# RWKV-7 keys transposed by VectorE and DMA instead of TensorE, in a two-layer streaming encoder step on one core

## The chip, the cores and the metric

One core of one Trainium2 chip runs the whole step. The metric is the device time of an execution in microseconds; the time given for the kernel before is the median of 3 executions. A profiled execution of the same kernel is looked at beside it.

## What is computed

The step has two layers over 512 prompt tokens and 32 sample tokens of width 1024, in float32. Layer 0 mixes tokens by RWKV-7 (24 heads of 64), layer 1 by differential attention; both also attend to a memory of 256 rows, multiply by a SiLU gate and project back. The change lies in layer 0. Its recurrence, per head, is

```python
def step(S, inp):
    r_t, k_t, v_t, w_t, kk_t, a_t = inp
    sa = jnp.einsum('bhvk,bhk->bhv', S, -kk_t)
    S = (S * w_t[:, :, None, :] + sa[..., None] * (kk_t * a_t)[:, :, None, :]
         + v_t[..., None] * k_t[:, :, None, :])
    return S, jnp.einsum('bhvk,bhk->bhv', S, r_t)
```

followed by a normalization of each head's output y (its mean taken off, then its variance), a bonus term, and the gate. The prompt starts from a zero state, the sample from `state_rwkv`; both last states are outputs.

## The kernel before

**Tiling.** The recurrence is done in chunks of 64 tokens: 8 for the prompt, and the sample's 32 tokens as a ninth. Two heads make a pair, so that 128 partitions are full; there are 12 pairs. For a pair, `rw_prep` turns projected rows into decayed queries and keys: `zr` and `bk` (features on partitions, tokens along the free dimension), the decay at each chunk's end `dl`, and the chunk matrices `at`. `rw_invert`, `rw_back`, `rw_at` and `rw_merge` invert the chunk matrices on GpSimd through DRAM scratch (`sc`, `m`). `rw_chain` runs `chunk` 8 times: each chunk reads the state `SB`, makes two matmuls into `ps_c`, an update `avz` by VectorE, a copy `sv` by ScalarE, then a matmul of `sv` with `bt` and the new `SB` by VectorE. This is the recurrence: three hops per chunk that wait for each other. `bt` is `bk` turned, tokens on partitions: for each half of the prompt (512 columns), four 128x128 transposes on TensorE into `ps_bt` and one copy `bt<-ps_bt` by ScalarE (lines 827 to 846). `rw_sample` does the same for the sample chunk, from a state `SS` that it loads at its begin (l. 994), transposes on TensorE (`ps_si`) and copies (`ssi`). `rw_finish` normalizes `yt`: `gs` is the sum over a head, scaled by 1/64, then subtracted.

**The projection in between.** TensorE's main work is the input projection `ps_g` (128x272 outputs). Each weight block of 1024x128 is loaded in two halves (`raw`), and split into a high part `whi` (a rounding copy by ScalarE) and a low part `wlo` (a subtraction by VectorE), so that a product is three matmuls in a row: `hh,whi`, `hl,whi`, `hh,wlo`, each half block 12 of them per half of the tokens. `stream` (in `layer0`) loads two blocks ahead and splits one ahead.

**What sets the order.** All engines work through queues in program order, and the program order is written by a planner in `layer0`. The main loop goes over the pairs; `PLAN` (l. 49) has 23 rows per pair with two halves each. A row issues one hop of the pair's recurrence and then the listed steps, for example `("prep", 2, 0, 0.42)`: the next step of `rw_prep` for the pair two ahead, with 0 us declared for TensorE and 0.42 us for VectorE. Between the steps it issues projection matmuls until a due time is reached. The steps of `rw_prep` are counted off by its `yield`s; the table says where each falls. A pair's last steps of `prep` come a pair or less ahead of its own chain: distance 2 in rows 13 to 15 and 0 to 14, distance 1 in rows 0 to 4 of the next pair.

The splits are deferred: `put_off` appends them to a list with 0.75 us declared for `wlo` (`LATER`) and 0 for `whi`, and `some` takes one from the list's head at the end of each half row, a `wlo` only if the room reckoned from the declared VectorE costs so far allows it (or if more than four wait). When a block's matmuls begin, `until(todo[-1][0])` issues whatever of that block's splits still stands in the list, at that place:

```python
    if self.later and 0 < self.later[0][1] <= room and self.place_no > self.acted + 1:
        fn, us = self.later.pop(0)
        fn()
...
    spent += self.some(room * (k + (half + 1) / 2) + 0.4 - spent)
```

SyncE issues nearly all DMAs, in order; a DMA whose data isn't ready holds up those behind it. Before the loop, three start-up stages (`FILL0` to `FILL2`) prepare pairs 0, 1 and 2 with projection blocks between. At pair 9 the kernel keeps back 24 projection steps (`KEPT`) for three last `prep` steps of pair 11.

All operations go through one helper (`tie`, l. 106), so the profile gives line 106 for nearly all, and they are told apart by the tiles' names.

Of the kernel before, what the change touches and what calls it, by code (L numbers as in the profile page):

```python
# [9 lines left out]
F32 = mybir.dt.float32  # L10
# [39 lines left out]
    [[("val", 0, 0.95, 0), ("prep", 2, 0.1, 0)], [("prep", 2, 0, 0.42)]],  # L50
# [14 lines left out]
    [[("fin", -1, 0, 0.98), ("smp", 0, 0.11, 0)], [("prep", 2, 0.4, 0), ("prep", 3, 0, 0.6)]],  # L65
# [8 lines left out]
SHIFTED, KEPT = 13, 24  # L74
# [34 lines left out]
class Trunk:  # L109
# [535 lines left out]
    def rw_prep(self, st, rkv):  # L645
# [73 lines left out]
        self.ve.tensor_copy(dl[:, :8], ch(de[:])[:, :, 64])  # L719
        self.ve.tensor_copy(dl[:, 8:9], de[:, CU - 1 : CU])  # L720
# [105 lines left out]
        self.ae.copy(sv[2][:TS, 0, :], ps[P - TS :, P : 2 * P])  # L826
        for q in range(2):
            yield
            if q:
                ps = self.psm.tile([P, 512], F32, tag="m", name="ps_v")  # L830
                for i in range(4):
                    self.te.transpose(ps[:, i * P : i * P + P], v[:, i * P : i * P + P], self.ident[:])
                pv = ps[:].rearrange("p (j c) -> p j c", j=4)
                for u in range(2):
                    if u:
                        yield
                    sv[u] = self.rb.tile([P, 4, P], F32, tag="sv", name="sv", bufs=4)
                    self.ae.copy(sv[u][:64, 0:4:2, :], pv[:64, 2 * u : 2 * u + 2])
                    self.ae.copy(sv[u][64:, 1:4:2, :], pv[64:, 2 * u : 2 * u + 2])
                yield  # L840
            ps = self.psm.tile([P, 512], F32, tag="m", name="ps_bt")
            for j in range(4):
                c = 4 * q + j
                self.te.transpose(ps[:, j * P : j * P + P], bk[:, c * P : c * P + P], self.ident[:])
            bt[q] = self.rb.tile([P, 4, P], F32, tag="bt", name="bt", bufs=4)
            self.ae.copy(bt[q][:], ps[:].rearrange("p (j c) -> p j c", j=4))
# [146 lines left out]

    def rw_sample(self, st):
# [3 lines left out]
        for h in range(2):  # L998
            self.se.dma_start(sl[64 * h : 64 * h + 64, 64 * h : 64 * h + 64], self.a["state_rwkv"][0, 0, 2 * pr + h])
# [1308 lines left out]
```

## Time and profile before

| what | value |
|---|---|
| median of 3 executions | 1348.16 us (1347.06 to 1348.51) |
| profiled execution, its own time | 1349.83 us |
| its span, first to last instruction | 1348.1 us |
| mean granted TensorE clock | 0.997 |
| TensorE matmul busy | 1319.8 us, 98% |
| VectorE busy | 956.5 us, 71% |
| ScalarE busy | 813.1 us, 60% |
| GpSimd busy | 368.0 us, 27% |
| moved by DMA | 150.47 MB, mean 112 GB/s |

The profile comes from one execution; its span is 1.7 us shorter than that execution's time. A row of a timeline has the start in us from the span's begin, the duration in us, the engine, the line, the operation and its tiles (output, then inputs), shapes, the count of equal instructions in the row, and in brackets, where the engine stood idle just before, how long and what released it. Matmuls overlap in TensorE's pipeline: the time that one costs the queue is the distance to the next one's start, not its duration. The layer-0 main loop lies at about 130 to 620 us, and a pair takes some 43.7 us of it (the same `wlo` starts at 236.67 and 280.29 us in two pairs that follow each other).

### The profile page before, as it was taken

The page shows a single profiled execution, that of the slowest core. Times are in us where ns is not written, and L with a number is a line of the kernel's source. Part 1 is how long each engine was busy: PE and PEld are TensorE (multiplying, and loading weights), DVE is VectorE, ACT ScalarE, POOL GpSimd, SP SyncE. Part 2 cuts the span into 40 slices and gives each one's busy share as a digit, 9 for nine tenths or more (in the row PEclk, how much of TensorE's full clock was granted, in tenths as well). Part 3 has the DMA queues.
Part 4 walks back from the last instruction along what each step waited for, and adds up shares of the span by engine and source line. Part 5 has one row for each costly group of instructions (what it writes and reads, how often), then busy time and mean ns, then how long its engine had stood idle before and what let it go on. Part 6 is the DMA issues. An engine that isn't in the chain of part 4 may idle for free. (4 is left out here: it accounts for less than half of the span.)

```text
span 1348.1 us, 31624 instructions
## 1 busy us (share of the span) xinstructions
PE 1319.8 (98%) x11662; PEld 1264.6 (94%) x11662; DVE 956.5 (71%) x2391; ACT 813.1 (60%) x2258; POOL 368.0 (27%) x833
## 2 busy tenths in 40 slices
PE   8999999999999999999999999999999999999997
PEld 6988899999999998988999999999999999999997
DVE  5766878888887888675764578876588748887343
ACT  5766777877787777665543366754476546664222
POOL 2128668666776677600000000000000001002000
PEclk9999999999999999999999999999999999999999
DMA  7443322333233322342465466652367424762321
GB/s 225 145 138 76 82 57 68 85 87 92 59 96 87 75 78 70 100 124 83 115 188 138 130 192 149 145 141 79 98 154 160 110 83 108 164 148 89 94 86 68
DMA packets 370805, 150.47 MB, mean 112 GB/s; under 512 B 163177, under 2 KB 361202, under 8 KB 370650
## 3 DMA queue, kind: packets, MB, share of 16 engines
q1 hardware_dynamic: 370586, 148.43, 42.0%
q8 instruction: 92, 1.51, 0.5%
q14 instruction: 63, 0.52, 0.1%
q10 hardware_dynamic: 64, 0.02, 0.0%
HBM read 118.00 MB, written 30.18 MB: 110 GB/s over the span
## 5 line engine op out<-in xcount | busy, mean ns | idle before, releaser
L106 PE MATMUL ps_g<-hh,wlo 128*128 128x272 f32 x1808 | 536.1, 297 | 1.1 <-DVE wlo L106 1.0
L106 PE MATMUL ps_g<-hh,whi 128*128 128x272 f32 x1808 | 533.9, 296 | 1.0 <-DVE ats L106 0.7
L106 PE MATMUL ps_g<-hl,whi 128*128 128x272 f32 x1808 | 532.7, 295 | 1.0 <-DVE hl L106 0.7
L106 PEld LDWEIGHTS ps_g<-hh,whi 128*128 128x128 f32 x1808 | 341.1, 189 | 5.9 <-DVE ats L106 0.9
L106 PEld LDWEIGHTS ps_g<-hl,whi 128*128 128x128 f32 x1808 | 340.9, 189 | 3.9 <-DVE hl L106 1.9
L106 PEld LDWEIGHTS ps_g<-hh,wlo 128*128 128x128 f32 x1808 | 340.5, 189 | 3.0 <-DVE wlo L106 1.8
L106 DVE TENSOR_TENSOR wlo<-raw,whi 128x512 fp32r<-128x512 f32 x314 | 214.4, 693 | 106.3 <-ACT whi L106 102.0
L106 ACT CAST whi<-raw 128x512 fp32r<-128x512 f32 x314 | 188.9, 619 | 116.7 <-PE ps_g L106 64.9
L868 POOL TENSOR_TENSOR tm<-u,m 102x84 f32<-102x84 f32 (+23 forms) x341 | 138.8, 407 | 117.6 <-DMA m<-sc 71.2
L870 POOL TENSOR_TENSOR u<-u,tm 102x84 f32<-102x84 f32 (+23 forms) x341 | 158.5, 465 | 26.7
L106 PE MATMUL ps_g<-hi,wlo 128*128 128x272 f32 x512 | 147.8, 289 | 1.1 <-DVE wlo L106 1.1
L106 PE MATMUL ps_g<-hi,whi 128*128 128x272 f32 x512 | 147.7, 288 | 0.0
L106 PE MATMUL ps_g<-lo,whi 128*128 128x272 f32 x512 | 147.4, 288 | 0.0
L1339 POOL TENSOR_TENSOR lo<-og,hi 128x544 fp32r<-128x544 f32 x8 | 13.2, 1651 | 378.1 <-ACT hi L106 377.6
L106 PEld LDWEIGHTS ps_g<-hi,wlo 128*128 128x128 f32 x512 | 96.4, 188 | 1.6 <-DVE wlo L106 1.5
L106 PEld LDWEIGHTS ps_g<-hi,whi 128*128 128x128 f32 x512 | 96.6, 189 | 0.0
L106 PEld LDWEIGHTS ps_g<-lo,whi 128*128 128x128 f32 x512 | 96.4, 188 | 0.0
L106 ACT ACTIVATE pt<-ps_s,snm 128x128 f32<-128x128 f32 (+3 forms) x96 | 50.3, 527 | 57.1 <-DVE snm L106 57.1
L106 DVE SCALAR_TENSOR_TENSOR SB<-ps_c,dl,sd 64x64 f32<-64x64 f32 x168 | 47.4, 282 | 26.6 <-PE ps_c L106 20.9
L106 ACT COPY sv<-ps_c 64x64 f32<-64x64 f32 x192 | 39.6, 206 | 33.1 <-PE ps_c L106 31.2
L1803 POOL MEMSET qs<- 128x128 f32 x2 | 0.3, 206 | 188.9 <-PE ps_g L106 188.9
L106 ACT ACTIVATE sg<-ps_g 128x272 f32<-128x272 f32 x64 | 25.1, 394 | 40.2 <-PE ps_g L106 36.2
(397 smaller groups left out, 2523.1 us busy)
## 6 DMA issues: line engine op xcount, KB each, us to landing
raw<-in_rw_in_dram SPq DMA_DIRECT2D x114, 256.0 KB
raw<-in_df_in_dram SPq DMA_DIRECT2D x112, 256.0 KB
raw<-in_w_out_dram SPq DMA_DIRECT2D x64, 256.0 KB
oscr<-sg SPq DMA_DIRECT2D x16, 272.0 KB
lo<-oscr SPq DMA_DIRECT2D x16, 272.0 KB
m<-sc SPq DMA_DIRECT2D x33, 128.0 KB
raw<-in_w_mem_v_dram SPq DMA_DIRECT2D x16, 256.0 KB
out_dram<-kt SPq DMA_DIRECT2D x48, 64.0 KB
```

The costliest lines, as they stand in the source:

```text
L106: return lambda *a, **k: self.trunk.tie(self, issue(*a, **k))
L868: nc.gpsimd.tensor_tensor(tm[:, :n, :wd], u3[:, :n, kx : kx + 1].to_broadcast(sh), m3[:, kx : kx + 1, kx + 1 :].to_broadcast(sh), ALU.mult)
L870: nc.gpsimd.tensor_tensor(u3[:, :n, kx + 1 :], u3[:, :n, kx + 1 :], tm[:, :n, :wd], ALU.add)
L1339: (self.nc.gpsimd if g % 2 and self.o1 else self.ve).tensor_tensor(lo[:], t, hi[:].bitcast(F32), ALU.subtract)
L1803: nc.gpsimd.memset(t[:], 0.0)
```

## The change

The eight prompt chunks' `bk` is no longer transposed on TensorE. VectorE transposes each half in squares of 32x32 within its 128x512 (two `STREAM_TRANSPOSE` per pair, row 0 of the pair before it is used). Each square is then right in itself but in the wrong place; four DMAs (`tscr<-bt`, one for each 32 partitions, 128-byte pieces) write the squares to DRAM where they belong, and one DMA (`bt<-tscr`) reads the whole 512 KB back. The writes are issued in row 0 right behind the transposes, the read-back in row 7. The copies `bt<-ps_bt` by ScalarE go with the transposes. `PLAN` declares 1.42 us of VectorE for the new step in place of 0.42 for the step that copied `dl`, and drops the two steps of rows 4 and 15 that held the TensorE transposes.

Besides, the `dl` and `ssi` copies move from VectorE to ScalarE; the scaling of `gs` is folded into the subtraction; the sample state `SS` is loaded in row 19 of the pair before; and the kept steps at pair 9 come in four portions instead of three.

```diff
--- before.py
+++ after.py
@@ -47,14 +47,14 @@
-    [[("val", 0, 0.95, 0), ("prep", 2, 0.1, 0)], [("prep", 2, 0, 0.42)]],
+    [[("val", 0, 0.95, 0), ("prep", 2, 0.1, 0)], [("prep", 2, 0, 0), ("prep", 1, 0, 1.42)]],
...
-    [[("smp", 0, 0.11, 0.28), ("prep", 1, 0.4, 0)], [("prep", 2, 0, 0.86)]],
+    [[("smp", 0, 0.11, 0.28)], [("prep", 2, 0, 0.86)]],
...
@@ -71,7 +71,7 @@
-SHIFTED, KEPT = 13, 24
+SHIFTED, ASKED, KEPT = 13, 19, 24
@@ -716,8 +716,8 @@
-        self.ve.tensor_copy(dl[:, :8], ch(de[:])[:, :, 64])
-        self.ve.tensor_copy(dl[:, 8:9], de[:, CU - 1 : CU])
+        self.ae.copy(dl[:, :8], ch(de[:])[:, :, 64])
+        self.ae.copy(dl[:, 8:9], de[:, CU - 1 : CU])
@@ -824,26 +824,29 @@
         bt[2] = self.rb.tile([P, 1, P], F32, tag="bts", name="bts", bufs=2)
         self.ae.copy(bt[2][:, 0, :], ps[:, :P])
         self.ae.copy(sv[2][:TS, 0, :], ps[P - TS :, P : 2 * P])
+        yield
+        scr = self.dp.tile([2 * TP, P], F32, tag="tscr", name="tscr", bufs=2)
+        tb = self.rb.tile([P, 8, P], F32, tag="bt", name="bt", bufs=2)
+        bt[:2] = tb[:, :4], tb[:, 4:]
         for q in range(2):
-            yield
-            if q:
-                ps = self.psm.tile([P, 512], F32, tag="m", name="ps_v")
-                for i in range(4):
-                    self.te.transpose(ps[:, i * P : i * P + P], v[:, i * P : i * P + P], self.ident[:])
-                pv = ps[:].rearrange("p (j c) -> p j c", j=4)
-                for u in range(2):
-                    if u:
-                        yield
-                    sv[u] = self.rb.tile([P, 4, P], F32, tag="sv", name="sv", bufs=4)
-                    self.ae.copy(sv[u][:64, 0:4:2, :], pv[:64, 2 * u : 2 * u + 2])
-                    self.ae.copy(sv[u][64:, 1:4:2, :], pv[64:, 2 * u : 2 * u + 2])
+            self.ve.transpose(bt[q].rearrange("p j c -> p (j c)"), bk[:, q * TP : q * TP + TP])
+        to = scr[:].rearrange("(b i) (a c) -> a i b c", i=TS, c=TS)
+        for a in range(4):
+            u = slice(TS * a, TS * a + TS)
+            self.se.dma_start(to[a], tb[u].rearrange("i j c -> i (j c)").rearrange("i (b c) -> i b c", c=TS))
+        yield
+        ps = self.psm.tile([P, 512], F32, tag="m", name="ps_v")
+        for i in range(4):
+            self.te.transpose(ps[:, i * P : i * P + P], v[:, i * P : i * P + P], self.ident[:])
+        pv = ps[:].rearrange("p (j c) -> p j c", j=4)
+        for u in range(2):
+            if u:
                 yield
-            ps = self.psm.tile([P, 512], F32, tag="m", name="ps_bt")
-            for j in range(4):
-                c = 4 * q + j
-                self.te.transpose(ps[:, j * P : j * P + P], bk[:, c * P : c * P + P], self.ident[:])
-            bt[q] = self.rb.tile([P, 4, P], F32, tag="bt", name="bt", bufs=4)
-            self.ae.copy(bt[q][:], ps[:].rearrange("p (j c) -> p j c", j=4))
+            sv[u] = self.rb.tile([P, 4, P], F32, tag="sv", name="sv", bufs=4)
+            self.ae.copy(sv[u][:64, 0:4:2, :], pv[:64, 2 * u : 2 * u + 2])
+            self.ae.copy(sv[u][64:, 1:4:2, :], pv[64:, 2 * u : 2 * u + 2])
+        yield
+        self.se.dma_start(tb[:], scr[:].rearrange("(j p) c -> p j c", p=P))
 
     def rw_invert(self, st):
 
@@ -991,17 +994,20 @@
             S, Sn = SB[c % 2], SB[(c + 1) % 2]
             yield from self.chunk(st, c, S, Sn)
 
+    def state_in(self, pr):
+
+        for h in range(2):
+            self.se.dma_start(self.SS[0][64 * h : 64 * h + 64, 64 * h : 64 * h + 64], self.a["state_rwkv"][0, 0, 2 * pr + h])
+
     def rw_sample(self, st):
 
         nc, p, pr = self.nc, self.rb2, st["pr"]
         sl = self.SS[0]
-        for h in range(2):
-            self.se.dma_start(sl[64 * h : 64 * h + 64, 64 * h : 64 * h + 64], self.a["state_rwkv"][0, 0, 2 * pr + h])
         yield
         ps = self.psm.tile([P, 4, P], F32, tag="m", name="ps_si")
         self.te.transpose(ps[:, 0, :], sl[:], self.ident[:])
         S = p.tile([P, P], F32, tag="ssi", name="ssi", bufs=1)
-        self.ve.tensor_copy(S[:], ps[:, 0, :])
+        self.ae.copy(S[:], ps[:, 0, :])
         yield from self.chunk(st, 8, S, sl)
         yield
         self.state_out(sl, self.o[8][0, 0, 2 * pr : 2 * pr + 2])
@@ -1097,10 +1103,9 @@
         y = yt[:].rearrange("p i (h v) -> p (i h) v", h=2)
         s = p.tile([P, 10], F32, tag="gs", name="gs", bufs=1)
         self.ve.tensor_reduce(s[:], y, AX.X, ALU.add)
-        self.ve.tensor_scalar(s[:], s[:], 1.0 / 64, None, ALU.mult)
         sh = [P, 10, 64]
         yield
-        self.ve.tensor_tensor(y, y, s[:].unsqueeze(2).to_broadcast(sh), ALU.subtract)
+        self.ve.scalar_tensor_tensor(y, s[:].unsqueeze(2).to_broadcast(sh), -1.0 / 64, y, ALU.mult, ALU.add)
         yield
         sq = p.tile([P, 10, 64], F32, tag="gsq", name="gsq", bufs=1)
         self.ae.activation(sq[:], y, AF.Square)
@@ -1615,6 +1620,7 @@
                 go(kind, 0)
                 fill(n)
             ready = len(FILL2) - 12
+            self.state_in(0)
             each[0] -= sum(map(sum, (FILL0, FILL1, FILL2, FILL3))) - 4 * 24 - 6 * 48
             for pr in range(NPAIR):
                 mplan = MPLAN.get(pr, ())
@@ -1648,6 +1654,8 @@
                                 t += MEMPE / 12
                         if half and pr == LAM and k in (1, 7):
                             (self.lam_in if k == 1 else self.lam_out)()
+                        if half and pr + 1 < NPAIR and k == ASKED:
+                            self.state_in(pr + 1)
                         if half and pr == NPAIR - 2 and k == SHIFTED:
                             self.shift_out()
                         if half and pr == NPAIR - 2 and k % 2 and len(came) < EARLY:
@@ -1665,9 +1673,9 @@
                     next(main)
                     left -= 1
                 if pr + 3 == NPAIR:
-                    for _ in range(3):
+                    for _ in range(4):
                         go("prep", pr + 2)
-                        fill(KEPT // 3)
+                        fill(KEPT // 4)
                     while self.later:
                         self.later.pop(0)[0]()
                     ca.close()
```

Three places of the queues follow. The first is VectorE's queue in a pair of the main loop, around rows 6 to 8 of the plan: `at` and `ats` are the chunk matrices, `SB` the state, `SS` the sample's state, `avz` the recurrence's update, `wlo` the low part of a weight half, `sg` a gate. Before:

```order
L106 TENSOR_TENSOR at_1695<-ps_at,mk 128x4x2x64 [waits PE_49] x2
L106 TENSOR_TENSOR avz<-ps_c,avz 64x128 [waits PE_49]
L106 TENSOR_TENSOR wlo<-raw,whi 128x512 [waits DMAHW4_49,Activation_49]
L106 TENSOR_TENSOR at_1695<-ps_at,mk 128x4x2x64 [waits PE_49] x2
L106 TENSOR_TENSOR ats<-ps_ats,mk 128x2x64 [waits PE_49] x2
L106 SCALAR_TENSOR_TENSOR SB_540<-ps_c,dl,sd 64x64 [waits PE_49,Activation_49]
L106 SCALAR_TENSOR_TENSOR SB_540<-ps_c,dl,sd 64x64
L106 SCALAR_TENSOR_TENSOR SS<-ps_c,dl,sd 64x64 [waits DMAHW6_49,PE_49]
L106 SCALAR_TENSOR_TENSOR SS<-ps_c,dl,sd 64x64 [waits DMAHW7_49]
L106 TENSOR_TENSOR avz<-ps_c,avz 64x128 [waits PE_49]
L106 TENSOR_TENSOR wlo<-raw,whi 128x512 [waits DMAHW5_49]
```

and in the changed kernel:

```order
L106 TENSOR_TENSOR at_1691<-ps_at,mk 128x4x2x64 [waits PE_49] x2
L106 TENSOR_TENSOR avz<-ps_c,avz 64x128 [waits PE_49]
L106 TENSOR_TENSOR at_1691<-ps_at,mk 128x4x2x64 [waits PE_49] x2
L106 TENSOR_TENSOR ats<-ps_ats,mk 128x2x64 [waits PE_49] x2
L106 SCALAR_TENSOR_TENSOR SB_540<-ps_c,dl,sd 64x64 [waits PE_49,Activation_49]
L106 SCALAR_TENSOR_TENSOR SB_540<-ps_c,dl,sd 64x64
L106 SCALAR_TENSOR_TENSOR SS<-ps_c,dl,sd 64x64 [waits DMAHW3_49,PE_49]
L106 SCALAR_TENSOR_TENSOR SS<-ps_c,dl,sd 64x64 [waits DMAHW4_49]
L106 TENSOR_TENSOR avz<-ps_c,avz 64x128 [waits PE_49]
L106 TENSOR_TENSOR wlo<-raw,whi 128x512 [waits DMAHW6_49]
L106 TENSOR_TENSOR wlo<-raw,whi 128x512 [waits DMAHW7_49,Activation_49]
```

The `wlo` that stood between `avz` and the second pair of `at` now stands behind the next `avz`, directly ahead of the block's other half. TensorE's third matmul of that block has a wait for VectorE there now; before it had none.

The second place is VectorE's queue some 13 us later in the same pair, rows 16 to 18: `q` and `nt` belong to a reciprocal square root, `yt` is the output being normalized, `bv` the bonus term. Before:

```order
L106 SCALAR_TENSOR_TENSOR q_101<-nt,q_101 128x26 [waits DVE_49]
L106 TENSOR_TENSOR yt_1689<-yt_1689,q_101 128x640 [waits DVE_49]
L106 TENSOR_TENSOR wlo<-raw,whi 128x512 [waits Activation_49]
L106 SCALAR_TENSOR_TENSOR SB_541<-ps_c,dl,sd 64x64 [waits PE_49,Activation_49]
L106 SCALAR_TENSOR_TENSOR SB_541<-ps_c,dl,sd 64x64
L106 MEMSET cum 128x9
L106 SCALAR_TENSOR_TENSOR bv_1690<-ps_y,PA,bv_1690 128x512 [waits PE_49]
L106 SCALAR_TENSOR_TENSOR bv_1690<-ps_y,PA,bv_1690 128x32 [waits PE_49]
L106 TENSOR_TENSOR avz<-ps_c,avz 64x128 [waits PE_49]
L106 TENSOR_TENSOR wlo<-raw,whi 128x512 [waits DMAHW7_49,Activation_49]
```

and in the changed kernel:

```order
L106 SCALAR_TENSOR_TENSOR q_101<-nt,q_101 128x26 [waits DVE_49]
L106 TENSOR_TENSOR wlo<-raw,whi 128x512 [waits Activation_49]
L106 TENSOR_TENSOR yt_1685<-yt_1685,q_101 128x640 [waits DVE_49]
L106 TENSOR_TENSOR wlo<-raw,whi 128x512 [waits DMAHW0_49,Activation_49]
L106 SCALAR_TENSOR_TENSOR SB_541<-ps_c,dl,sd 64x64 [waits PE_49,Activation_49]
L106 SCALAR_TENSOR_TENSOR SB_541<-ps_c,dl,sd 64x64
L106 MEMSET cum 128x9
L106 SCALAR_TENSOR_TENSOR bv_1686<-ps_y,PA,bv_1686 128x512 [waits PE_49]
L106 SCALAR_TENSOR_TENSOR bv_1686<-ps_y,PA,bv_1686 128x32 [waits PE_49]
L106 TENSOR_TENSOR avz<-ps_c,avz 64x128 [waits PE_49]
```

The `wlo` that stood behind `avz` now stands ahead of `yt`, and two stand between `nt` and `SB` where one stood.

The third place is SyncE's queue in the start-up: `m` and `sc` belong to the inverse of pair 0, `raw` are halves of weight blocks, `memt` and `mkv` memory keys. Before:

```order
L106 DMA m_1165<-sc_1146 32x1024
L106 DMA m_1165<-sc_1146 2x1024
L106 DMA raw<-in_rw_in_dram 128x4x128 x2
L106 DMA out_dram<-memt 128x2x128
L106 DMA mkv_781<-memt 128x256
L106 DMA raw<-in_rw_in_dram 128x4x128 x2
```

and in the changed kernel:

```order
L106 DMA m_1165<-sc_1146 32x1024
L106 DMA m_1165<-sc_1146 2x1024
L106 DMA tscr<-bt 32x32x32 x4
L106 DMA bt<-tscr 128x8x128
L106 DMA raw<-in_rw_in_dram 128x4x128 x2
L106 DMA out_dram<-memt 128x2x128
L106 DMA mkv_781<-memt 128x256
L106 DMA raw<-in_rw_in_dram 128x4x128 x2
```

The four scratch writes and the read-back for pair 0 stand ahead of a load of weights. In the main loop the writes stand ahead of a load of weights too, and the read-back two loads later.

More of the change, by code (lines that the diff above doesn't have):

```diff
@@ L53 @@
     [[("prep", 2, 0, 0)], [("prep", 2, 0, 1.0)]],
-    [[("smp", 0, 0.11, 0.28), ("prep", 1, 0.4, 0)], [("prep", 2, 0, 0.86)]],
+    [[("smp", 0, 0.11, 0.28)], [("prep", 2, 0, 0.86)]],
     [[("out", -1, 0.11, 0)], [("prep", 2, 0, 0.84)]],
     [[("prep", 2, 0, 1.1), ("smp", 0, 0.21, 0.29)], [("prep", 2, 0, 0.86)]],
-    [[("prep", 2, 1.1, 1.37)], [("smp", 0, 0.21, 0)]],
+    [[("prep", 2, 1.1, 1.37)], [("smp", 0, 0.21, 0), ("prep", 1, 0, 0)]],
     [[], [("prep", 2, 0, 0.9), ("prep", 2, 1.1, 1.37)]],
@@ L64 @@
     [[("prep", 2, 0.25, 0)], []],
-    [[("fin", -1, 0, 0.98), ("smp", 0, 0.11, 0)], [("prep", 2, 0.4, 0), ("prep", 3, 0, 0.6)]],
+    [[("fin", -1, 0, 0.98), ("smp", 0, 0.11, 0)], [("prep", 3, 0, 0.6)]],
     [[("prep", 3, 0.53, 0), ("mrg", 1, 0, 0.86)], []],
```

## The prediction

> **What bounds the kernel now.** I read the page's engine totals first, then the table by stretches for the layer-0 main loop (about 130 to 620 us, where most of the change acts).
>
> ```profile
> span 1348.1 us, 31624 instructions
> PE 1319.8 (98%) x11662; PEld 1264.6 (94%) x11662; DVE 956.5 (71%) x2391; ACT 813.1 (60%) x2258; POOL 368.0 (27%) x833
> ...
> L106 PE MATMUL ps_g<-hh,wlo 128*128 128x272 f32 x1808 | 536.1, 297 | 1.1 <-DVE wlo L106 1.0
> ```
>
> ```profile
> 250.00:300.00 50.00, 50.00 (x549) 47.64 (x549) 42.15 (x105) 38.41 (x112) 35.39 (x74) 1.00 0.28 72
> ```
>
> In the stretch from 250 to 300 us the columns are PE, PEld, DVE, ACT, POOL, granted clock, DMA share, GB/s: TensorE is busy for all 50.00 us at clock 1.00, VectorE for 42.15, ScalarE for 38.41. So TensorE's issue is the bound: work taken from it shortens the stage, and any wait put into its queue lengthens it, unless a pause is already there. The group's line on the page says that in the whole run TensorE waits only 1.0 us for wlo, the low half of a split weight. That will matter: the planner gives VectorE's splits their places.
>
> **What TensorE is relieved of.** The 24 groups of four transposes go. To see their worth I read TensorE's timeline at two groups of one pair, by the starts of neighbours, not by durations, since matmuls overlap.
>
> ```profile
> L106 PE MATMUL ps_bt<-ident,bk x96: 270/272/330, 83.1 to 562.0; 128*128 128x128 f32 x96
> ```
>
> ```profile
> 222.83 0.27 PE L106 MATMUL ps_si<-ident,SS 128*128 128x128 f32 x1
> 222.94 0.60 PE L106 MATMUL ps_bt<-ident,bk 128*128 128x128 f32 x4
> 223.29 0.37 PE L106 MATMUL ps_g<-hh,whi 128*128 128x272 f32 x1
> ...
> 244.54 0.60 PE L106 MATMUL ps_bt<-ident,bk 128*128 128x128 f32 x4
> 244.90 0.37 PE L106 MATMUL ps_g<-hl,whi 128*128 128x272 f32 x1
> 245.11 0.29 PE L106 MATMUL ps_g<-hh,wlo 128*128 128x272 f32 x1
> ```
>
> The first group takes 223.29 - 222.94 = 0.35 us of issue. ps_si stays ahead of it, so the longer step into the main projection (0.21 us instead of about 0.125) stays too. The second stands alone between projection matmuls: 0.36 us, and the step 245.11 - 244.90 = 0.21 falls by 0.085, together 0.445. Twelve pairs: 12 x 0.35 + 12 x 0.445 = **9.5 us gained**. The durations would promise more: 24 groups of 0.60 us are 14.4.
>
> [...]
>
> **First new wait: a split forced at the block's start.** The order shows VectorE's queue changed beyond what the diff names. Once per pair, in pairs 1 to 8, the first-half wlo of a projection block stood after an avz at row 6; now it stands behind the next avz, directly ahead of its second half, because the higher VectorE cost declared for row 0 (1.42 in place of 0.42) leaves a deferred split less room at that place, and the block's start then forces what is left. These are the rows of before, TensorE and then VectorE.
>
> ```profile
> 235.85 0.46 PE L106 MATMUL ps_c<-SB,zr 128*128 128x128 f32 x2
> 236.06 0.37 PE L106 MATMUL ps_g<-hh,wlo 128*128 128x272 f32 x1
> 236.27 0.29 PE L106 MATMUL ps_g<-hh,whi 128*128 128x272 f32 x1
> 236.40 0.29 PE L106 MATMUL ps_g<-hl,whi 128*128 128x272 f32 x1
> 236.53 0.29 PE L106 MATMUL ps_g<-hh,wlo 128*128 128x272 f32 x1
> ```
>
> ```profile
> 231.35 0.67 DVE L106 TENSOR_TENSOR wlo<-raw,whi 128x512 fp32r<-128x512 f32 x1
> ...
> 236.34 0.29 DVE L106 TENSOR_TENSOR avz<-ps_c,avz 64x128 f32<-64x128 f32 x1
> 236.67 0.69 DVE L106 TENSOR_TENSOR wlo<-raw,whi 128x512 fp32r<-128x512 f32 x1
> ```
>
> The block's third matmul, at 236.53, reads that wlo, done since 232.0 in before. In the new order the split comes where the second-half wlo stands now, at 236.67, behind an avz that waits for the ps_c of 235.85. It ends at 236.67 + 0.69 = 237.36; TensorE wants it at 236.53. That is a wait of 0.83 us, or 0.96 with the 0.13 us that a hand-over from VectorE can take (252.83 to 252.96, below). Everything in TensorE's queue stands behind it, and so does the recurrence. I take 0.9 us x 8 pairs = **7.2 us lost** (bounds 0 if a pause elsewhere absorbed it, and 7.7; rows of before show no such pause).
>
> **Second new wait: a split ahead of the state.** A wlo that stood at 254.03, after the state update, now goes ahead of yt, in pairs 1 to 7.
>
> ```profile
> 246.10 0.58 DVE L106 SCALAR_TENSOR_TENSOR SB<-ps_c,dl,sd 64x64 f32<-64x64 f32 x2 [1.25 <-PE ps_c L106]
> ...
> 250.77 0.83 DVE L106 TENSOR_TENSOR yt<-yt,q 128x640 f32<-128x640 f32 x1
> 251.51 0.83 DVE L106 TENSOR_TENSOR wlo<-raw,whi 128x512 fp32r<-128x512 f32 x1
> 252.26 0.57 DVE L106 SCALAR_TENSOR_TENSOR SB<-ps_c,dl,sd 64x64 f32<-64x64 f32 x2
> ...
> 254.03 0.67 DVE L106 TENSOR_TENSOR wlo<-raw,whi 128x512 fp32r<-128x512 f32 x1
> ```
>
> ```profile
> 252.84 0.29 PE L106 MATMUL ps_g<-hh,whi 128*128 128x272 f32 x1
> 252.96 0.42 PE L106 MATMUL ps_c<-SB,zr 128*128 128x128 f32 x2
> ```
>
> VectorE waits for TensorE ahead of the SB at 246.10, and from there no row has an idle time up to the SB that ends at 252.83. TensorE's ps_c follows at 252.96, just one matmul step after 252.84: no margin, but no wait yet. One more split costs its step, 252.26 - 251.51 = 0.75 us; leaving a hand-over's few hundredths of slack, 0.7 us x 7 = **4.9 us lost** (0 to 5.3).
>
> **What VectorE, ScalarE and the queue take on.** For the squares the trace has a layer-1 transpose of the same 128x512 shape, on row 0 of the next pair an idle time, and behind it the copies that leave.
>
> ```profile
> L106 DVE STREAM_TRANSPOSE kt<-k x12: 711/711/711, 811.9 to 1196.8; 128x512 f32<-128x512 f32 x12
> ```
>
> ```profile
> 215.40 0.24 DVE L106 COPY dl<-de 128x8 f32<-128x8 f32 x2
> 217.47 0.58 DVE L106 TENSOR_SCALAR SB<-ps_c,dl 64x64 f32<-64x64 f32 x2 [1.82 <-PE ps_c L106]
> ...
> 261.09 0.58 DVE L106 TENSOR_SCALAR SB<-ps_c,dl 64x64 f32<-64x64 f32 x2 [1.71 <-PE ps_c L106]
> ```
>
> Two transposes take 2 x 0.711 = 1.42 us and stand right ahead of that SB. The idle time is 1.71 to 1.82, and the dl copies (0.24) leave it: some 0.5 us of cover remains, so I cost them at nothing; without the cover it would be 1.42 x 11 = 16 us. The copies given to ScalarE (dl, ssi) go against its 24 dropped copies of ps_bt; it has 11.6 of 50 us free. The dropped scaling of gs and the earlier state load are off the path: nothing.
>
> On SyncE's queue, four scratch writes (128 KB each, in 128-byte pieces) now stand ahead of a weight load in every pair and wait for the transposes. Rows of before, the load and the split that needs it, and the nearest small-piece writes with the read that waits for them:
>
> ```profile
> 258.26 1.14 SPq L106 DMA_DIRECT2D raw<-in_rw_in_dram  x2
> ...
> 829.66 3.42 SPq L106 DMA_DIRECT2D ascr<-og  x4
> 833.19 1.01 SPq L106 DMA_DIRECT2D raw<-in_df_in_dram  x2
> 834.67 0.37 SPq L106 DMA_DIRECT2D og<-ascr  x1
> ```
>
> ```profile
> 271.64 0.60 ACT L106 CAST whi<-raw 128x512 fp32r<-128x512 f32 x1
> ```
>
> The transposes end before 261.1; the writes' issue takes up to 3.42 us, so the load goes out near 264.5 instead of 258.26, 7.1 us ahead of its use. The read-back is asked for seven rows after the writes, and has most of a pair until it is used. Both hidden: nothing, with a few tenths per pair at the worst in the range.
>
> [...]
>
> In the start-up there is less room. For pair 0 the writes and the read-back stand together, ahead of a weight load; these are the queue, then its reader, then TensorE.
>
> ```profile
> 84.08 2.02 SPq L106 DMA_DIRECT2D m<-sc  x6
> 86.20 1.30 SPq L106 DMA_DIRECT2D raw<-in_rw_in_dram  x2
> ```
>
> ```profile
> 94.48 0.62 ACT L106 CAST whi<-raw 128x512 fp32r<-128x512 f32 x1
> ```
>
> ```profile
> 84.54 0.66 PE L106 MATMUL ps_v<-ident,rkv 128*128 128x128 f32 x4 [0.59 <-ACT svs L106]
> ...
> 99.11 0.73 PE L106 MATMUL ps_b<-r,hs 128*128 128x128 f32 x5 [0.72 <-ACT r L106]
> ```
>
> Issuing four writes takes 1.35 us at the pitch of the m reads (2.02 us for six) and up to 3.42 by the row of ascr; waiting until they have landed takes 834.67 - 833.08 = 1.6 us or more; the read-back's issue 0.4. The load leaves 3.4 to 5.4 us late, with 2.9 to 4.9 us until its use at 94.48. ScalarE would stand there with the start of pair 0 behind it (r, for which TensorE already waits at 99.11). Bounds: a gain of 0.6 (the wait at 84.54 goes with the ps_bt copies) to a loss of 5.4; I take a net loss of **1.4 us**, since the load has most of the time it needs.
>
> **The sum.** -9.5 + 7.2 + 4.9 + 1.4 = +4.0 us. The profiled execution took 1349.83 us (1.7 more than its span); 1353.8 of that kind is 1348.16 + 4.0 = **1352.2 us** against the median.
>
> **The rivals.** (1) *The relief is kept*: one of the two split waits is absorbed, by a place where the recurrence, not the issue, sets TensorE's pace. For it: the 24 groups surely go. Against it: rows of before show no pause of 0.7 us after either place. With the first wait gone, 1352.2 - 7.2 = 1345.0; with both, 1340.1. Chance 0.19. This one ends faster; it decides from the point where over 6.7 us of the waits are absorbed. (2) *Nearly nothing*: the start-up costs nothing and the waits come out at their lower prices, 0.83 x 8 + 0.6 x 7 = 10.8 against 9.5 + 0.6: +0.7, or 1348.9 us. Chance 0.28. (3) *Transfers*: the scratch writes land so slowly that the weight load misses its use in every pair. Each microsecond past the 7.1 costs 11 us in 11 pairs: 1352.2 + 11 = 1363. For it: the start-up load in before was issued 8.3 us ahead of its use, so no row proves 7.1 enough. Against it: a DMA share of 0.28. Chance 0.10. (4) *Durations count*: 14.4 instead of 9.5 is gained, 1352.2 - 4.9 = 1347.3; the 0.35 us between neighbours speaks against it. Chance 0.03. [...] That the transposes don't leave TensorE can't be: the new order has none.
>
> **How the numbers follow.** My forecast has 0.40, and its own range is 1351 to 1356. A measurement of this kernel tells 0.2%, 2.7 us, from no change, so faster is below 1345.5 and slower above 1350.9. Faster is rival 1 and a sliver of rival 4: 0.20. Same is rival 2 and the rest of rival 4: 0.30. Slower is the forecast and rival 3: 0.50. The range reaches into rival 1 and over rival 2, and leaves out 1340 and the far transfers: 1342 to 1358.
>
> **What would show it.** Right: no ps_bt rows; in each of pairs 1 to 8 a matmul ps_g<-hh,wlo with an idle time of about 0.9 us released by DVE wlo, and the group's 1.1 us of idle time grown to about 8; in pairs 1 to 7 a ps_c<-SB with 0.7 us of idle time released by DVE SB; TensorE busy under 50 of 50 us in every stretch of the loop; the SB at the pair's begin still with idle time ahead of it. Wrong: these waits at under 0.3 us, a pair shorter than before by 0.8 us, or waits for DMA raw on ScalarE inside the loop.

## The result, and the profile after

| kernel | median | ratio to before, 95% interval |
|---|---|---|
| before | 1348.34 us (4 runs) | |
| changed | 1366.68 us (1364.55 to 1368.89, 4 runs) | 1.0137 (1.0118 to 1.0157) |

The change costs 18.5 us (15.9 to 21.2), on the side that was forecast, but 14.5 us more than forecast and outside the range. These are the head of the changed kernel's page and the group of matmuls that need the low halves of weights.

```profile
span 1366.9 us, 31492 instructions
PE 1318.2 (96%) x11566; PEld 1259.5 (92%) x11566; DVE 964.0 (71%) x2367; ACT 806.7 (59%) x2270; POOL 356.9 (26%) x833
...
L106 PE MATMUL ps_g<-hh,wlo 128*128 128x272 f32 x1808 | 540.7, 300 | 6.9 <-DVE wlo L106 6.7
```

TensorE is busy for 96% in place of 98%: its busy time fell by 1.6 us and the span grew by 18.8. The idle time ahead of the low-half matmuls rose from 1.1 to 6.9 us, as the order had said. That is a third of the loss. The list of TensorE's waits names the rest: engine, tile and line, what it waited for, us in total, times, the longest.

```profile
PE ps_g L106 <- DVE wlo L106: 8.1, 12, 1.0
PE ps_b L106 <- ACT r L106: 5.8, 1, 5.8
PE ps_ck L106 <- DMA cmt<-in_cache_mem_k_dram: 5.4, 1, 5.4
...
PE ps_y L106 <- DVE yt L106: 1.4, 5, 0.4
```

Two single waits of 5.8 and 5.4 us stand there, once each in the run. To see when the time is lost I compared the starts of the same instruction in both traces (changed minus before, us):

| instruction, its start in before | lag |
|---|---|
| ps_rt of pair 0's preparation, 96.9 | -0.3 |
| ps_s of pair 1's preparation, 119.0 | +6.3 |
| ps_si of pair 1, 179.1 | +5.9 |
| ps_si of pair 8, 485.5 | +11.1 |
| ps_bts of pair 11's preparation, 545.7 | +12.8 |
| ps_si of pair 10, 571.2 | +20.0 |
| first ps_sc of layer 1, 814.9 | +19.5 |

So there are three losses: 6.6 us in one place of the start-up, 5.1 us spread over seven pairs of the main loop (0.73 a pair), and 7.3 us in one place at pair 9. Between the last two stand another 1.7 us. There pair 9 has a split ahead of SB too, and TensorE waits twice:

```profile
549.77 0.39 PE L106 MATMUL ps_g<-hh,whi 128*128 128x272 f32 x1 [0.80 <-DVE ats L106]
...
552.25 0.65 PE L106 MATMUL ps_c<-SB,zr 128*128 128x128 f32 x2 [1.14 <-DVE SB L106]
```

```profile
552.00:556.00 4.00, 3.75 (x16) 3.62 (x17) 2.23 (x6) 0.57 (x4) 0.22 (x1) 0.57 0.36 58
```

The third column from the right of the last row is the clock that TensorE was granted, a share of full speed. It is 0.57 in these 4 us (0.50 in each stretch of 1 us from 553 to 555), so half of full speed for 3.4 of them, and that is most of the 1.7 us: in the first kernel of the experiments (the later transfers) the same splits stand at the same places, TensorE waits 1.2 us for that SB, the clock stays at 1.00, and the lag there grows by 0.2 us. The two profiled executions differ by 19.1 us, since that of the changed kernel took 1368.89 us. The first place, in the changed kernel, on SyncE's queue, ScalarE and TensorE:

```profile
86.71 3.35 SPq L106 DMA_DIRECT2D tscr<-bt  x4
94.02 0.38 SPq L106 DMA_DIRECT2D bt<-tscr  x1
94.49 1.19 SPq L106 DMA_DIRECT2D raw<-in_rw_in_dram  x2
```

```profile
99.20 0.62 ACT L106 CAST whi<-raw 128x512 fp32r<-128x512 f32 x1 [4.95 <-DMA raw<-in_rw_in_dram]
```

```profile
103.87 1.25 PE L106 MATMUL ps_b<-r,hs 128*128 128x128 f32 x5 [5.79 <-ACT r L106]
```

The read-back may not go out before the four writes have landed; it goes out 4.0 us after the last issue (90.06 to 94.02), and this is meant here by the time to land. The load behind it goes out at 94.49 in place of 86.20 and needs another 4.7 us until ScalarE can start at 99.20. In ScalarE's queue r stands behind that split, in both kernels, so r, which has nothing to do with that load, comes 4.8 us late too (103.55 in place of 98.80), and with it TensorE. The second place is the kept stage at pair 9, where pair 11 is prepared: SyncE, then TensorE.

```profile
574.44 2.69 SPq L106 DMA_DIRECT2D tscr<-bt  x4
579.83 0.38 SPq L106 DMA_DIRECT2D bt<-tscr  x1
580.25 0.57 SPq L106 DMA_DIRECT2D cmt<-in_cache_mem_k_dram  x1
```

```profile
584.26 0.66 PE L106 MATMUL ps_ck<-ident,cmt 128*128 128x128 f32 x2 [5.36 <-DMA cmt<-in_cache_mem_k_dram]
584.57 0.58 PE L106 MATMUL ps_g<-hh,wlo 128*128 128x272 f32 x1
584.95 0.43 PE L106 MATMUL ps_g<-hh,whi 128*128 128x272 f32 x1
585.17 0.43 PE L106 MATMUL ps_g<-hl,whi 128*128 128x272 f32 x1
```

It is the same figure: writes, read-back, and the load that TensorE needs next behind them. The last two rows show something more. The matmuls behind the wait take 0.43 us and follow each other after 0.22 us, in place of 0.29 and 0.125. The table by stretches has the reason in the granted clock (the first figure behind the length is TensorE's busy time, with its matmuls):

```profile
100.00:105.00 5.00, 1.13 (x6) 1.13 (x6) 3.60 (x5) 3.80 (x10) 4.45 (x8) 0.68 0.94 271
105.00:110.00 5.00, 5.00 (x28) 5.00 (x29) 3.30 (x7) 2.33 (x6) 4.37 (x9) 0.63 0.19 57
110.00:115.00 5.00, 5.00 (x49) 4.73 (x47) 3.91 (x7) 1.07 (x3) 4.37 (x9) 1.00 0.20 56
...
585.00:590.00 5.00, 5.00 (x21) 4.64 (x21) 0.42 (x1) 2.32 (x7) 1.11 (x5) 0.51 0.57 191
590.00:595.00 5.00, 5.00 (x39) 4.90 (x39) 3.63 (x9) 2.00 (x8) 0.00 (x0) 1.00 0.04 10
```

At each of the two long waits the clock is at half for 6.8 us (0.50 in each stretch of 1 us from 102 to 108 and from 584 to 589). It falls while TensorE still waits (at 101.8 and 583.1 us), so that 4.8 and 5.7 us of it lie behind the wait: 28 and 21 matmuls in 5 us, where it does 49 and 39 at clock 1.00.

In the main loop each of pairs 1 to 8 shows the first wait that the prediction had worked out. First TensorE at the block's start, then VectorE at the pair's begin:

```profile
242.69 0.29 PE L106 MATMUL ps_g<-hl,whi 128*128 128x272 f32 x1
243.71 0.40 PE L106 MATMUL ps_g<-hh,wlo 128*128 128x272 f32 x1 [0.73 <-DVE wlo L106]
```

```profile
222.18 1.30 DVE L106 STREAM_TRANSPOSE bt<-bk 128x512 f32<-128x512 f32 x2
224.12 0.58 DVE L106 TENSOR_SCALAR SB<-ps_c,dl 64x64 f32<-64x64 f32 x2 [0.63 <-PE ps_c L106]
```

The step from 242.69 to 243.71 is 1.02 us where 0.126 would do: 0.89 us lost. The bracket says 0.73, because it counts from the end of the matmul before; steps between starts are what the queue loses. The transposes at the pair's begin leave 0.63 us of idle time ahead of SB, so they are covered.

### The profile page after: what moved, and what is told of

The parts are those of the page before. It is cut to its first block, busy times and chain, and to the rows that moved or that the text cites. A ratio compares the mean times of both kernels' runs of the same rounds, so it can differ in the third digit from the quotient of the medians.

```text
span 1366.9 us, 31492 instructions
## 1 busy us (share of the span) xinstructions
PE 1318.2 (96%) x11566; PEld 1259.5 (92%) x11566; DVE 964.0 (71%) x2367; ACT 806.7 (59%) x2270; POOL 356.9 (26%) x833
## 5 line engine op out<-in xcount | busy, mean ns | idle before, releaser
L871 POOL TENSOR_TENSOR tm<-u,m 102x84 f32<-102x84 f32 (+23 forms) x341 | 143.6, 421 | 115.5 <-DMA m<-sc 68.5
L873 POOL TENSOR_TENSOR u<-u,tm 102x84 f32<-102x84 f32 (+23 forms) x341 | 145.0, 425 | 26.7
```

Of the source, the lines that this page charges most:

```text
L871: nc.gpsimd.tensor_tensor(tm[:, :n, :wd], u3[:, :n, kx : kx + 1].to_broadcast(sh), m3[:, kx : kx + 1, kx + 1 :].to_broadcast(sh), ALU.mult)
L873: nc.gpsimd.tensor_tensor(u3[:, :n, kx + 1 :], u3[:, :n, kx + 1 :], tm[:, :n, :wd], ALU.add)
```

## The experiments

Theory Q: the loss has two parts. SyncE's queue holds needed loads behind a read-back at two places, each followed by half clock; and the splits stand at places where TensorE waits for them. Rivals: R, the recurrence sets a pair's pace, and a wait removed comes back at the next hop; S, the scratch traffic slows everything; V, the transposes fit only because the splits moved away. All times are compared by the ratio to the kernel before on the same chip, since medians of before went from 1348.3 to 1350.1 us between chips.

### Transfers of pairs 0 and 11 later

```diff
-SHIFTED, ASKED, KEPT = 13, 19, 24
+SHIFTED, ASKED, KEPT, LATEBACK = 13, 19, 24, (0, 11)
...
+        if st["pr"] in LATEBACK:
+            st["write"] = write
+        else:
+            write()
...
+                if k == 9:
+                    sts[0]["write"]()
+                if k == 20:
+                    sts[0]["back"]()
...
+                        if half and pr == NPAIR - 2 and k == 0:
+                            sts[11]["write"]()
+                        if half and pr == NPAIR - 2 and k == 5:
+                            sts[11]["back"]()
```

> Only the transfers of pairs 0 and 11 move: their four scratch writes and their read-back are issued later, behind the loads that stood behind them. Theory Q (the queue's wait and the clock after it, at these two places, cost 6.6 and 7.9 us, the forced splits the rest): 1366.7 - 14.5 = 1352.2 us, 1350 to 1354; ScalarE no longer waits 4.95 us for raw nor TensorE 5.4 us for cmt. Rival S (the scratch traffic of all pairs slows everything; a wait removed comes back elsewhere): 1362 to 1367.

Measured: 1356.96 us, ratio 1.0052 (1.004 to 1.0064); 11.5 us of the 18.5 are gone. Both waits are gone. ScalarE's split starts at the time of before, with no idle time ahead of it:

```profile
94.38 0.62 ACT L106 CAST whi<-raw 128x512 fp32r<-128x512 f32 x1
```

S falls: the same bytes still move in every pair. It is 11.5 and not 14.5, and the time is outside the forecast's 1350 to 1354: in the start-up the lag is -0.65 us at 119.0 and +2.3 at 179.1. In between TensorE waits 1.14 and 0.87 us for the inverse of pair 0 (below), and the clock is at half for 6.8 us there, in before for 3.4.

A kernel that moves only the two read-backs, and leaves the writes where they are:

```diff
-        self.se.dma_start(tb[:], scr[:].rearrange("(j p) c -> p j c", p=P))
+
+        def back():
+            self.se.dma_start(tb[:], scr[:].rearrange("(j p) c -> p j c", p=P))
+
+        if st["pr"] in LATEBACK:
+            st["back"] = back
+        else:
+            back()
```

> Only the read-backs of pairs 0 and 11 are issued later; their writes stay ahead of the loads. Theory Q (the read-back's wait holds the queue): ScalarE's wait for raw falls from 4.95 to under 1.5 us, TensorE's for cmt from 5.4 to 2 to 3, and the time from 1366.7 to 1355 to 1359. If the writes' issue (3.35 and 2.7 us) holds it: 1362 or more.

Measured: 1358.05 us, ratio 1.006 (1.0048 to 1.0072), 10.4 us gone. The waits of ScalarE and of TensorE:

```profile
93.78 0.62 ACT L106 CAST whi<-raw 128x512 fp32r<-128x512 f32 x1 [0.27 <-DMA raw<-in_rw_in_dram]
```

```profile
574.02 0.41 PE L106 MATMUL ps_ck<-ident,cmt 128*128 128x128 f32 x2 [1.86 <-DMA cmt<-in_cache_mem_k_dram]
```

4.95 us became 0.27, 5.36 became 1.86. So it is the read-back's wait for the landing that holds the queue, not the issue of the writes; only at pair 11 do the writes' 2.5 us of issue cost something too.

### Splits back in their places

```diff
-    ... ("prep", 1, 0, 1.42)]],
+    ... ("prep", 1, 0, 1.0)]],
```

> VectorE's declared cost in row 0 is 1.0 instead of 1.42, which gives the first-half split of the third block its old place in 8 pairs and leaves the split ahead of yt and the one of pair 9 where they are. Theory Q: 8 waits of 0.89 us go, 1366.7 - 7.1 = 1359.6, 1358 to 1361. Rival R (the recurrence, not TensorE's issue, sets the pace of a pair, so what one wait gives the next hop takes back): 1364 or more.

Measured: 1363.63 us, ratio 1.0109 (1.0092 to 1.0125): 3.8 us gone, not 7.1. The waits for wlo at the block's start are gone, but two others grew (TensorE's waits of this kernel):

```profile
PE ps_c L106 <- DVE SB L106: 3.0, 5, 0.8
PE ps_y L106 <- DVE yt L106: 2.6, 8, 0.6
PE ps_g L106 <- DVE wlo L106: 2.2, 4, 1.0
```

Over the seven pairs the lag grows by 0.13 us a pair in place of 0.73: 0.60 of the 0.89 us stay gained. (With the split, one `whi` of ScalarE and one `sg` of VectorE change their places in seven of these pairs.) R is right in a part: where TensorE no longer waits at the block's start, it waits more behind the second split. With a declared cost of 0.42 both splits are back in pairs 1 to 8:

```diff
-    ... ("prep", 1, 0, 1.42)]],
+    ... ("prep", 1, 0, 0.42)]],
```

> The declared cost is 0.42: all splits stand as in the kernel before. Theory Q: 7.1 for the block's start, 7 x 0.72 = 5.0 for the split ahead of the state and about 1.2 for pair 9: 1366.7 - 13.3 = 1353.4, 1351.5 to 1355. Rival R: above 1361. Rival V (the two transposes don't fit the pause of row 0 unless the splits are moved away): waits of TensorE for SB at the pair's begin, and 1356 or more.

Measured: 1358.56 us, ratio 1.0063 (1.0049 to 1.0077): 10.0 us gone. The lag falls by 0.76 us a pair (8.7 at ps_si of pair 1, 3.4 at that of pair 8), near what a pair's two groups of transposes were forecast to be worth (0.795). No wait for SB appears in the loop, and the transposes leave the same 0.63 us of idle time ahead of SB; V falls, and so does R as the main cause. Less than 13.3 was gained. In this trace the start-up has another 10 us of half clock near 140 us, and the lag goes there from 6.4 us at 119.0 to 8.7 at 179.1 (in the changed kernel from 6.3 to 5.9), which may be the difference.

Both edits together, the later transfers (the first diff) and 0.42:

> Both together. Theory Q: 1366.7 - 14.5 - 13.3 = 1338.9, 1337 to 1341, that is the kernel before less the 9.5 us of transposes. Rivals R and S: 1346 or more.

Measured: 1344.26 us, ratio 0.996 (0.9948 to 0.9972): 5.4 us less than before. This is the version that beats both kernels. It stands between the forecasts, 3 us above theory Q's 1341 at most and below the rivals' 1346: Q counted the relief at 9.5 us, and the next section has what it is worth. The stretch whose row of before the prediction shows is this, in the changed kernel and in this one:

```profile
250.00:300.00 50.00, 48.76 (x526) 45.90 (x526) 41.09 (x98) 37.60 (x113) 31.51 (x71) 1.00 0.42 98
```

```profile
250.00:300.00 50.00, 49.89 (x571) 47.46 (x571) 43.52 (x104) 38.74 (x115) 35.67 (x75) 1.00 0.40 98
```

TensorE busy for 48.76 of 50 us, and 49.89 again, with the DMA share as high (0.40, before 0.28). The transfers alone cost the loop nothing that shows.

### What the relief is worth

```diff
-            ps = self.psm.tile([P, 512], F32, tag="m", name="ps_bt")
-            for j in range(4):
-                c = 4 * q + j
-                self.te.transpose(ps[:, j * P : j * P + P], bk[:, c * P : c * P + P], self.ident[:])
-            bt[q] = self.rb.tile([P, 4, P], F32, tag="bt", name="bt", bufs=4)
-            self.ae.copy(bt[q][:], ps[:].rearrange("p (j c) -> p j c", j=4))
+            bt[q] = self.ident[:].unsqueeze(1).to_broadcast([P, 4, P])
```

> The kernel before without the 24 groups of transposes and their 24 copies; the recurrence multiplies by the identity in place of the turned keys, and nothing else moves. By the distance of neighbours (0.35 and 0.445 us a group): 9.5 us less than before, 8.5 to 10.5. By durations (0.60 us a group): 14.4 less. Rival R (the recurrence sets a pair's pace): 0 to 4 less.

Measured: 1345.68 us, ratio 0.9968 (0.9956 to 0.998): 4.3 us less (2.7 to 5.9), not 9.5, and close to the 0 to 4 that rival R gave. But in the loop the gain is there: the lag goes from -0.2 us at ps_si of pair 1 to -4.3 at that of pair 8. In the start-up it was given back (-1.5 at 119.0, -0.2 at 179.1), at this wait of TensorE for the inverse of pair 0:

```profile
128.06 0.22 PE L106 MATMUL ps_w<-t1b,at 32*32 32x32 f32 x2 [1.86 <-DVE t1b L106]
```

Behind pair 8 nothing is added either (-4.3, then -4.7 at layer 1). The small edits alone, all but the fourth portion of the kept steps, which has no run of its own:

```diff
-        self.ve.tensor_copy(dl[:, :8], ch(de[:])[:, :, 64])
+        self.ae.copy(dl[:, :8], ch(de[:])[:, :, 64])
...
-        self.ve.tensor_copy(S[:], ps[:, 0, :])
+        self.ae.copy(S[:], ps[:, 0, :])
...
-        self.ve.tensor_scalar(s[:], s[:], 1.0 / 64, None, ALU.mult)
...
+                        if half and pr + 1 < NPAIR and k == ASKED:
+                            self.state_in(pr + 1)
```

> The kernel before with the small edits alone: dl and ssi copied by ScalarE, the scaling of gs folded, SS loaded a pair ahead; transposes, plan and transfers as before. Forecast: no change, within 1.5 us of before. Rival (they carry part of the loss, since ScalarE's copies come late for the state): 2 us or more slower.

Measured: 1348.91 us, ratio 0.9993 (0.9984 to 1.0003). No difference that can be told.

### Size of the pieces

```diff
-        bt[:2] = tb[:, :4], tb[:, 4:]
+        bt[:2] = [self.ident[:].unsqueeze(1).to_broadcast([P, 4, P])] * 2
...
-        to = scr[:].rearrange("(b i) (a c) -> a i b c", i=TS, c=TS)
+        to = scr[:].rearrange("(a i r) c -> a i (r c)", a=4, i=TS)
...
-            self.se.dma_start(to[a], tb[u].rearrange("i j c -> i (j c)").rearrange("i (b c) -> i b c", c=TS))
+            self.se.dma_start(to[a], tb[u].rearrange("i j c -> i (j c)"))
```

> The changed kernel, its scratch writes in pieces of 4 KB that are not placed; the recurrence multiplies by the identity, the transposes, four writes and one read-back of the same bytes stay. Theory P (the 128-byte pieces make the wait for landing, 4.0 us in the start-up): the read-back goes out within 2 us of the writes, ScalarE's wait for raw falls from 4.95 to under 3 us, and the time by 4 to 8 us to about 1360. Theory L (a latency of the round trip, whatever the pieces): the wait stays over 4 us and the time at 1364 to 1368.

Measured: 1363.13 us, ratio 1.0097 (1.0084 to 1.011), 5.4 us under the changed kernel. SyncE and ScalarE in the start-up:

```profile
86.53 2.54 SPq L106 DMA_DIRECT2D tscr<-bt  x4
92.21 0.38 SPq L106 DMA_DIRECT2D bt<-tscr  x1
```

```profile
97.44 0.62 ACT L106 CAST whi<-raw 128x512 fp32r<-128x512 f32 x1 [3.35 <-DMA raw<-in_rw_in_dram]
```

The writes are issued in 2.54 us in place of 3.35 and land 3.1 us behind the last issue in place of 4.0; the wait is 3.35 us in place of 4.95. At pair 9 the landing falls from 2.7 to 1.9 us and TensorE's wait for cmt from 5.4 to 3.6, with 3.4 us at half clock in place of 6.8. This is between the theories: the small pieces cost 1.6 to 1.8 us a round, and the rest of the wait is there with pieces of 4 KB too. In the loop they cost nothing that shows (the lag grows by 0.79 us a pair, with small pieces by 0.73).

### Pauses of a known length

```diff
+        ps = self.psm.tile([P, 512], F32, tag="m", name="ps_z")
+        for i in range(4):
+            self.te.transpose(ps[:, i * P : i * P + P], self.ident[:], self.ident[:])
+        for _ in range(n):
+            self.ve.tensor_scalar(ps[:], ps[:], 1.0, None, ALU.mult)
+        self.te.transpose(ps[:, :P], self.ident[:], self.ident[:])
```

> The kernel before, in whose main loop TensorE is made to wait for 1, 3, 5 and 8 VectorE operations on one accumulator bank (some 0.7 us each) in pairs 2, 4, 6 and 8, far from any other wait: pauses of about 1.0, 2.4, 3.8 and 5.9 us, 13 us in all. [...] Rival U (the dips belong to the start-up's small matmuls, not to pauses): the clock stays 1.00 in the main loop, 1361 to 1362.

Measured: 1370.5 us, ratio 1.015 (1.0135 to 1.0165), 20.2 us more. TensorE's pauses, and the stretches around the second, third and fourth:

```profile
235.22 0.33 PE L106 MATMUL ps_z<-ident 128*128 128x128 f32 x1 [0.79 <-DVE ps_z L106]
325.90 0.33 PE L106 MATMUL ps_z<-ident 128*128 128x128 f32 x1 [2.26 <-DVE ps_z L106]
417.97 0.48 PE L106 MATMUL ps_z<-ident 128*128 128x128 f32 x1 [3.73 <-DVE ps_z L106]
514.46 0.47 PE L106 MATMUL ps_z<-ident 128*128 128x128 f32 x1 [5.93 <-DVE ps_z L106]
```

```profile
320.00:330.00 10.00, 7.74 (x70) 7.05 (x69) 7.50 (x17) 3.71 (x12) 4.97 (x12) 1.00 0.24 41
410.00:420.00 10.00, 6.27 (x52) 5.76 (x52) 7.08 (x13) 3.15 (x11) 5.20 (x14) 0.81 0.20 32
420.00:430.00 10.00, 10.00 (x69) 9.84 (x68) 7.64 (x19) 5.28 (x14) 4.35 (x12) 0.85 0.43 106
510.00:520.00 10.00, 5.54 (x30) 5.55 (x31) 6.41 (x13) 0.95 (x3) 1.01 (x3) 0.66 0.58 129
```

With 0.79 and 2.26 us the clock stays 1.00. With 3.73 and 5.93 us it falls to half for 6.8 us each, by the rows above (2 x (0.19 + 0.15) x 10 and 2 x 0.34 x 10). Read in stretches of 1 us, it falls at 416.2 and 511.8 us, inside the pauses, so that 5.1 and 4.2 us of it lie behind them. By the starts of ps_si the pairs with the last three pauses lose 2.9, 6.6 and 8.4 us, where the steps across the pauses are 2.9, 4.5 and 6.7: the half clock costs 2.1 and 1.7 us. The clock doesn't stay at 1.00 in the main loop (0.81, 0.85 and 0.66 in the rows above), and the time is over U's 1361 to 1362: U falls, as far as it says that only small matmuls do this.

### Three tries to mend the start-up

Pair 1's writes and read-back moved into the main loop as well:

```diff
-SHIFTED, ASKED, KEPT, LATEBACK = 13, 19, 24, (0, 11)
+SHIFTED, ASKED, KEPT, LATEBACK = 13, 19, 24, (0, 1, 11)
...
-                        if half and pr == NPAIR - 2 and k == 0:
-                            sts[11]["write"]()
+                        if half and pr in (0, NPAIR - 2) and k == 0:
+                            sts[pr + 1]["write"]()
```

> As the kernel with the splits' old places and the late transfers of pairs 0 and 11 (1344.3), and pair 1's writes and read-back go into pair 0 of the main loop too, behind the loads of its inverse, which they held up by 2.7 us. Theory Q: TensorE's wait of 1.8 us at ps_w goes, 1344.3 - 2.6 = 1341.7, 1340 to 1343. Rival (what is left there is the granted clock, which dips near 130 us in the kernel before too): 1343.5 to 1345.5.

Measured: 1345.84 us, ratio 0.9962 (0.995 to 0.9975); TensorE's wait at ps_w is still 1.80 us. The rival holds: those writes were not what it waited for. Steps of the projection moved in front:

```diff
-FILL2 = [4, 6, 6, 6, 2, 2, 0, 4, 0, 6, 2, 6, 4, 6]
+FILL2 = [4, 12, 12, 6, 2, 2, 0, 4, 0, 0, 2, 0, 4, 6]
```

> As the kernel with the splits' old places and the late transfers of pairs 0 and 11 (1344.3), and 12 of the start-up's projection steps are issued ahead of ps_w, where TensorE waits 1.8 and 0.8 us for the inverse of pair 0, instead of behind it. Theory I (in that stage the inverse, by GpSimd and DMA, sets the pace, so that matmuls ahead of ps_w are free): 1344.3 - 1.5 to 2.6, and less again by 1.7 where the half clock behind the pause goes: 1340 to 1343. Rival (the matmuls delay what the inverse needs): 1344 or more.

Measured: 1348.54 us, ratio 0.9986 (0.9977 to 0.9995), slower by 0.26% than without the edit. The 12 steps stood ahead of ps_w before too, so that the edit only shifted them within the stage, and the wait grew to 3.5 us; it doesn't try the theory. The kernel that does:

```diff
-FILL2 = [4, 6, 6, 6, 2, 2, 0, 4, 0, 6, 2, 6, 4, 6]
+FILL2 = [4, 6, 6, 6, 2, 2, 0, 4, 0, 6, 2, 6, 4, 18]
```

> As the kernel with the splits' old places and the late transfers of pairs 0 and 11 (ratio to before 0.996), and the start-up's last stage takes 12 projection steps more, just ahead of ps_w, which pair 0 of the main loop then lacks. (The kernel tried before only moved steps about within that stage.) Theory I (there the inverse of pair 0, not TensorE, sets the pace): the waits of 1.8 and 0.8 us at ps_w shrink by about 1.5 us, the time by 1.5 to 3: ratio 0.994 to 0.995. Rival (the steps come late for something else, or the half clock eats the gain): 0.996 or more.

Measured: 1349.51 us, ratio 1.0001 (0.9992 to 1.001). The first waits at ps_w shrink to 0.30 and 0.67 us, and the next one, of ps_w for ScalarE's t1b, is 2.25:

```profile
134.20 1.06 PE L106 MATMUL ps_w<-at,t1b 32*32 32x32 f32 x32 [2.25 <-ACT t1b L106]
```

The rival holds, and the time is 0.4% over the kernel without the edit. That a chain through the inverse sets the pace there fits all three, but none of them made the stage shorter. The half clock near 130 us lasts 13.7, 10.2 and 10.2 us in these three traces, and 3.4 in the kernel that they start from and in before. One execution of the first of the three, at a mean clock of 0.998 where the other five had 0.993 to 0.996, took 1340.43 us, as theory Q had forecast. So the half clock may have hidden what that edit gains there; how much of the stage it is stays open.

## Why the prediction was wrong

**The direction and the main loop were right.** 0.89 us for the split at the block's start (0.9 forecast), and a net of +0.73 us a pair against 0.9 + 0.7 - 0.795 = +0.8. The two splits together cost 10.0 us where the queue's waits stay and 12.4 where they don't (1.0052 against 0.996), 12.1 forecast. What was not seen is that the two share a slack: the second alone costs 0.89 us a pair (0.13 + 0.76), not 0.7, and the first beside it adds 0.60. The sign that was named for the second is missing: pairs 1 to 7 of the changed kernel have no wait of ps_c for SB, but 1.2 us of ps_y for yt in four of them; the wait for SB appears where the second split stands alone. (The 1.0 us that the prediction gives for all of before is that of one group of matmuls; the list of TensorE's waits has 3.1 us for wlo.)

**Transposes, copies and the transfers of the main loop at nothing: right.** 0.63 us of cover was left (some 0.5 forecast), with the splits in their old places too; the small edits change nothing, and with splits and queue mended the loop runs at 49.89 of 50 us.

**The step that failed is the one on the start-up**: "I take a net loss of 1.4 us, since the load has most of the time it needs." It measured 6.6 us. Three things are in it. The landing was taken from a read-back of another kind at 1.6 us "or more" (that row bounds it from above, since the read-back went out then) and is 4.0, so that the load left 8.3 us late (94.49 against 86.20), not 3.4 to 5.4. How long a weight load needs from its issue to its use had no row, and was taken as less than the 2.9 to 4.9 us that were left; it is 4.7. With that much lateness and that much need, ScalarE stood 4.7 us late (99.20 against 94.48). And this wait of 5.8 us had a tail: 4.8 us at half clock behind it, some 1.5 us more. The bound of 5.4 us was near the wait itself by luck, for it let the load leave 2.9 us earlier than it did and gave it no room at all until its use; the value of 1.4 chosen within it had nothing under it.

**A place was left out of the sum.** Pair 11 is prepared in the kept stage, where the writes and the read-back follow each other with TensorE's next load behind them, as in the start-up. "For pair 0 the writes and the read-back stand together" is true of two pairs. 5.4 us of wait and some 2 of half clock came from there: 7.3, where the sum had nothing.

**The relief was counted over all pairs.** "Twelve pairs" gave 9.5; the kernel without the transposes gains 4.3. The rate per pair is near (0.59 us measured in the kernel without the transposes, 0.76 in the one with both splits back, 0.795 forecast), but it counts only where TensorE sets the pace; in the start-up the gain was given back at ps_w.

**Rival 3 had the mechanism's name and the wrong place**: a load that misses its use, but in two places, not in every pair. With what the kernels showed (relief and the rest of the change -5.4, splits 12.4, queue with half clock 13.9) the sum is 20.9 against 18.5 measured. Each price is that of mending one part with the other mended already, and the 2.4 between the sums is what the two parts share (splits 12.4 or 10.0); it is no more than the intervals, some 2 to 3 us wide for each difference, so whether they share anything is not shown.

## What to carry to other kernels

In the start-up the read-back that waited for the writes' landing held the load behind it on SyncE's queue (issued at 94.49 us in place of 86.20); when such a DMA is added, look at each place where it is issued, the irregular ones above all, for the load that comes next and when that is needed. A gain per loop turn counts only for the turns in which that engine sets the pace (4.3 us here, where all turns would give 9.5). A planner's cost figures move other instructions than the one they describe: one figure, set to the true duration, put two splits where TensorE waits for them, and a wrong one is faster by 10 us. Half clock alone cost 2.1 and 1.7 us behind two pauses, as much as some differences between two traces, so read the granted clock of each stretch before a wait is blamed.

## What the hardware showed

In these kernels a long pause of TensorE was paid twice. In the kernel with pauses 0.79 and 2.26 us left the clock at 1.00; pauses of 3.73, 5.4, 5.8 and 5.93 us came with 6.8 us at half clock, of which 4.2 to 5.7 us lay behind the pause, worth 2.1 and 1.7 us where it was measured. The stretches at half clock lasted 3.4 us (near 131 us in before), 6.8, 10.2, and 13.7 in one kernel. The length of a wait doesn't tell it alone: in the kernel with late read-backs a wait of 1.86 us was followed by some 3.4 us at half clock, in the changed kernel waits of 0.80 and 1.14 us close to each other were, and before shows such a stretch near 131 us with no wait over 0.5 us ahead of it, among matmuls of 32x32. What decides it is not shown.

In the scratch writes the 128-byte pieces landed later: 4.0 us behind the last issue, against 3.1 in pieces of 4 KB, for the same 512 KB in the start-up, and 2.7 against 1.9 at pair 9, that is 22 to 30% of the landing.
